# Grouped softmax: tiles of 384 rows in four buffers instead of 256 rows in six

## The chip, the cores and the metric

The kernel runs on one core of one Trainium2 chip. Times are device microseconds of one execution; the time of a kernel is the median of its runs. Before the change it is 1327.28 us (three runs, 1326.36 to 1327.6). The profile shows one execution, of 1324.7 us.

Three engines and the transfers matter here. VectorE (DVE in the profile) takes maxima and scales, ScalarE (ACT) takes exponentials, and two engines only issue transfers: SyncE (SP) the loads and GpSimd (POOL) most of the stores. The transfers themselves run on 16 DMA engines, which both queues share.

## What is computed

```python
def setup_inputs():
    B, N, D, G = 4, 4096, 4352, 8
    return {"x": np.random.randn(B, N, D).astype(np.float32)}

def reference(x):
    B, N, D = x.shape
    G = 8
    Dg = D // G
    x_g = x.reshape(B, N, G, Dg)
    x_g = x_g - x_g.max(axis=-1, keepdims=True)
    exp = np.exp(x_g)
    out = exp / exp.sum(axis=-1, keepdims=True)
    return out.reshape(B, N, D).astype(np.float32)
```

There are 4 x 4096 = 16,384 rows of 4352 float32 values (17,408 B). Each row is cut into eight groups of 544 values, and each group gets its own softmax. 285.2 MB are read and as many are written.

## The kernel before

A tile is 256 rows: each of the 128 partitions holds R = 2 whole rows that lie next to each other in memory, 34,816 B, and one DMA packet brings them. There are 64 tiles, and NT = 6 buffers that are used in turn. A tile is loaded into its buffer, worked on in place, and stored from it; the buffer is loaded again once its store has landed.

```python
    R = 2
    NT = 6
    RG = R * G
    ...
    xt = xf.rearrange("(t p r) d -> t p (r d)", p=P, r=R)
    ...
    bufs = [ctx.enter_context(nc.sbuf_tensor(f"xt{b}", [P, R * D], f32)) for b in range(NT)]
    ...
    parts = [(t, slice(0, RG)) for t in range(nt - 1)]
    parts += [(nt - 1, slice(r * G, (r + 1) * G)) for r in range(R)]
```

A part is a whole tile (16 groups per partition); only the last tile is done as two parts of one row each. VectorE takes the negated maxima of a part in one instruction, and later the reciprocals of the sums and the scaling, one instruction each:

```python
    def vector_max(n):
        t, g = parts[n]
        i = nc.vector.reduce_max(
            out=mx[:, t % NT, g], in_=groups(t, g), axis=X, negate=True)
        if g.start == 0:
            i.wait_op(landed[t % NT], 16 * (t // NT + 1), "sem-ge")
        ...
        i.then_inc(max_done, 1)

    def vector_scale(n):
        t, g = parts[n]
        nc.vector.reciprocal(out=rs[:, t % NT, g], in_=sm[:, t % NT, g]).wait_op(
            exp_done, n + 1, "sem-ge").then_inc(rec_done, 1)
        xg = groups(t, g)
        nc.vector.tensor_tensor(
            out=xg,
            in0=xg,
            in1=rs[:, t % NT, g].unsqueeze(2).to_broadcast([P, g.stop - g.start, Dg]),
            op=mybir.AluOpType.mult,
        ).wait_op(rec_done, n + 1, "sem-ge").then_inc(scaled, 1)
```

ScalarE takes one activation per group: exp(x - max), with the sum of the group as a second output.

```python
    def scalar_exp(n, count):
        ...
        for g in range(gs.start, gs.stop):
            i = nc.scalar.activation(
                out=xg[:, g - gs.start, :], in_=xg[:, g - gs.start, :], func=Exp,
                bias=mx[:, t % NT, g:g + 1], scale=1.0,
                accum_out=sm[:, t % NT, g:g + 1])
            if g == gs.start:
                i.wait_op(max_done, count, "sem-ge")
        i.then_inc(exp_done, 1)
```

The order is: SyncE issues all loads, each after the store that frees its buffer, and the stores of the last two tiles; GpSimd issues the other stores. ScalarE runs in a loop over the six buffers. VectorE runs straight through all tiles, and takes the maxima of tile n + 1 ahead of the scaling of tile n, so that ScalarE has work while VectorE scales:

```python
    for t in range(nt):
        if t >= NT:
            nc.sync.wait_ge(stored[t % NT], 16 * (t // NT))
        ...
            nc.sync.dma_start(out=tile_in[:, :], in_=xt[t]).then_inc(landed[t % NT], 16)
        ...
    for t in range(nt - LAST):
        nc.gpsimd.wait_ge(scaled, t + 1)
        nc.gpsimd.dma_start(out=ot[t], in_=bufs[t % NT][:, :]).then_inc(stored[t % NT], 16)
    ...
    vector_max(0)
    for n in range(len(parts)):
        if n + 1 < len(parts):
            vector_max(n + 1)
        vector_scale(n)
```

Of the kernel before, what the change touches and what calls it, by code (L numbers as in the profile page):

```python
# [1 line left out]

# [4 lines left out]


@with_exitstack
def kernel(  # L10
    ctx: ExitStack,
    tc: tile.TileContext,
    x: bass.AP,
    out: bass.AP,
):
    nc = tc.nc
    G = 8
    P = 128
    R = 2
    NT = 6  # L20
    RG = R * G
    xf = x.flatten_outer_dims()
    of = out.flatten_outer_dims()
    N, D = xf.shape
    Dg = D // G
    nt = N // (P * R)
    LAST = 2
    FIRST = 2
    turns = (nt - 1 - FIRST) // NT
    f32 = mybir.dt.float32  # L30
    X = mybir.AxisListType.X
    Exp = mybir.ActivationFunctionType.Exp
    xt = xf.rearrange("(t p r) d -> t p (r d)", p=P, r=R)
    ot = of.rearrange("(t p r) d -> t p (r d)", p=P, r=R)

    landed = [tc.alloc_semaphore(f"landed{b}") for b in range(NT)]
    stored = [tc.alloc_semaphore(f"stored{b}") for b in range(NT)]
    last_landed = tc.alloc_semaphore("last_landed")
    last_stored = tc.alloc_semaphore("last_stored")


    max_done = tc.alloc_semaphore("max_done")
    exp_done = tc.alloc_semaphore("exp_done")
    rec_done = tc.alloc_semaphore("rec_done")
    scaled = tc.alloc_semaphore("scaled")

    ctx.enter_context(tc.tile_critical(  # L47
        sync_engine=mybir.EngineType.Pool, no_gpsimd_drain=True))
    bufs = [ctx.enter_context(nc.sbuf_tensor(f"xt{b}", [P, R * D], f32)) for b in range(NT)]
    mx = ctx.enter_context(nc.sbuf_tensor("mx", [P, NT, RG], f32))  # L50
    sm = ctx.enter_context(nc.sbuf_tensor("sm", [P, NT, RG], f32))
    rs = ctx.enter_context(nc.sbuf_tensor("rs", [P, NT, RG], f32))

    parts = [(t, slice(0, RG)) for t in range(nt - 1)]
    parts += [(nt - 1, slice(r * G, (r + 1) * G)) for r in range(R)]

    def groups(t, g):
        return bufs[t % NT][:, :].rearrange("p (g d) -> p g d", d=Dg)[:, g, :]

    def vector_max(n):  # L60
        t, g = parts[n]
        i = nc.vector.reduce_max(  # L62
            out=mx[:, t % NT, g], in_=groups(t, g), axis=X, negate=True)
        if g.start == 0:
            i.wait_op(landed[t % NT], 16 * (t // NT + 1), "sem-ge")
        else:
            i.wait_op(last_landed, 16, "sem-ge")
        i.then_inc(max_done, 1)

    def vector_scale(n):  # L70
        t, g = parts[n]
        nc.vector.reciprocal(out=rs[:, t % NT, g], in_=sm[:, t % NT, g]).wait_op(  # L72
            exp_done, n + 1, "sem-ge").then_inc(rec_done, 1)
        xg = groups(t, g)
        nc.vector.tensor_tensor(  # L75
            out=xg,
            in0=xg,
            in1=rs[:, t % NT, g].unsqueeze(2).to_broadcast([P, g.stop - g.start, Dg]),
            op=mybir.AluOpType.mult,
        ).wait_op(rec_done, n + 1, "sem-ge").then_inc(scaled, 1)  # L80

    def scalar_exp(n, count):
        t, gs = parts[n]
        xg = groups(t, gs)
        for g in range(gs.start, gs.stop):
            i = nc.scalar.activation(  # L86
                out=xg[:, g - gs.start, :],
                in_=xg[:, g - gs.start, :],
                func=Exp,
                bias=mx[:, t % NT, g:g + 1],  # L90
                scale=1.0,
                accum_out=sm[:, t % NT, g:g + 1],
            )
            if g == gs.start:
                i.wait_op(max_done, count, "sem-ge")
        i.then_inc(exp_done, 1)

    for t in range(nt):  # L100
        if t >= NT:
            nc.sync.wait_ge(stored[t % NT], 16 * (t // NT))
        tile_in = bufs[t % NT]
        if t < nt - 1:
            nc.sync.dma_start(out=tile_in[:, :], in_=xt[t]).then_inc(landed[t % NT], 16)  # L105
        else:
            for r in range(R):
                nc.sync.dma_start(
                    out=tile_in[:, r * D:(r + 1) * D], in_=xt[t, :, r * D:(r + 1) * D],
                ).then_inc(landed[t % NT] if r < R - 1 else last_landed, 16)  # L110
    for t in range(nt - LAST, nt):
        nc.sync.wait_ge(scaled, t + 1 if t < nt - 1 else len(parts))
        nc.sync.dma_start(out=ot[t], in_=bufs[t % NT][:, :]).then_inc(last_stored, 16)


    for t in range(nt - LAST):
        nc.gpsimd.wait_ge(scaled, t + 1)
        nc.gpsimd.dma_start(out=ot[t], in_=bufs[t % NT][:, :]).then_inc(stored[t % NT], 16)  # L118
    for t in range(nt - NT, nt - LAST):
        nc.gpsimd.wait_ge(stored[t % NT], 16 * (t // NT + 1))  # L120
    nc.gpsimd.drain()
    nc.gpsimd.wait_ge(last_stored, 16 * LAST)

    nc.scalar.preload_act_table(Exp)  # L124

    for n in range(FIRST):
        scalar_exp(n, n + 1)
    nc.scalar.sem_inc(max_done, -FIRST)
    with nc.scalar.Fori(0, turns):
        for k in range(NT):  # L130
            scalar_exp(FIRST + k, k + 1)
        nc.scalar.sem_inc(max_done, -NT)
    for k, n in enumerate(range(FIRST + turns * NT, len(parts))):
        scalar_exp(n, k + 1)


    vector_max(0)
    for n in range(len(parts)):
        if n + 1 < len(parts):
            vector_max(n + 1)  # L140
        vector_scale(n)


# [1 line left out]
_INS = ['x']  # L145
_OUTS = [((4, 4096, 4352), 'float32')]


# [23 lines left out]
```

## Time and profile before

| what | value |
|---|---|
| time, median of 3 runs | 1327.28 us |
| span of the profiled run | 1324.7 us |
| bytes moved, mean rate | 570.48 MB, 431 GB/s over the span |
| maxima of a two-row tile (VectorE) | 9219 ns each |
| scaling of a two-row tile (VectorE) | 9225 ns each |
| reciprocals of a two-row tile (VectorE) | 243 ns each |
| exponentials of one group (ScalarE) | 734 ns each, 1024 of them |
| load of a tile, issue to landing (median) | 32.4 us |
| store of a tile, issue to landing (median) | 51.5 us |

How to read it: the busy time of an engine is only the time of its instructions. An engine may be busy for most of the span and still not be what the others wait for. So one asks at every stage which wait ends last, and what would start earlier if it were shorter. A row of forty digits shows the busy share of forty equal slices of the span in tenths (9 is 90% or more). A queue's share is the time that its packets took, as a share of what 16 DMA engines could give in the span. In the lists of waits a line is "who waited for what: us in total, times, the longest".

### The profile page before, as it was taken

The page shows a single profiled execution, that of the slowest core. Times are in us where ns is not written, and L with a number is a line of the kernel's source. Part 1 is how long each engine was busy: PE and PEld are TensorE (multiplying, and loading weights), DVE is VectorE, ACT ScalarE, POOL GpSimd, SP SyncE. Part 2 cuts the span into 40 slices and gives each one's busy share as a digit, 9 for nine tenths or more (in the row PEclk, how much of TensorE's full clock was granted, in tenths as well). Part 3 has the DMA queues.
Part 4 walks back from the last instruction along what each step waited for, and adds up shares of the span by engine and source line. Part 5 has one row for each costly group of instructions (what it writes and reads, how often), then busy time and mean ns, then how long its engine had stood idle before and what let it go on. Part 6 is the DMA issues. An engine that isn't in the chain of part 4 may idle for free.

```text
span 1324.7 us, 2465 instructions
## 1 busy us (share of the span) xinstructions
DVE 1190.0 (90%) x195; ACT 757.4 (57%) x2049; POOL 33.3 (3%) x66
## 2 busy tenths in 40 slices
DVE  5999999988989889898898998988989889898893
ACT  3765566547456465564655646556465474654751
POOL 0000000000000000000000000000000000000000
DMA  9999999999999999999999999999999999999998
GB/s 404 421 434 433 432 432 434 434 432 431 435 435 432 430 434 437 432 432 432 436 434 430 433 435 433 431 433 435 433 433 431 434 436 432 431 432 437 432 432 372
DMA packets 18582, 570.48 MB, mean 431 GB/s; under 512 B 2064, under 2 KB 2064, under 8 KB 2064
## 3 DMA queue, kind: packets, MB, share of 16 engines
q1 hardware_dynamic: 9648, 294.13, 51.5%
q0 software_dynamic: 8928, 276.30, 48.3%
q14 instruction: 6, 0.05, 0.0%
HBM read 285.21 MB, written 285.21 MB: 431 GB/s over the span
## 4 chain that ended last, share of the span: by engine, by line
another core or an unknown queue 69%; DVE 20%; DMA 7%; ACT 1%; SPq 1%; issue 0%; POOLq 0%
DVE xt L75 10%; DVE mx L62 10%; DMA out_dram<-xt 4%; DMA xt<-in_x_dram 3%; ACT xt L86 1%; SPq L105 1%; DVE rs L72 0%; SPq L167 0%; POOLq L47 0%; POOLq L156 0%
## 5 line engine op out<-in xcount | busy, mean ns | idle before, releaser
L86 ACT ACTIVATE xt<-xt,mx 128x544 f32<-128x544 f32 x1024 | 750.1, 734 | 542.4 <-DVE mx L62 542.4
L62 DVE TENSOR_REDUCE mx<-xt 128x16 f32<-128x8704 f32 (+1 forms) x65 | 590.1, 9079 | 110.8 <-DMA xt<-in_x_dram 110.8
L75 DVE TENSOR_TENSOR xt<-xt,rs 128x8704 f32<-128x8704 f32 (+1 forms) x65 | 590.6, 9086 | 2.2
L86 ACT ACTIVATION_READ_ACCUMULATOR xt<-xt,mx 128x1 f32 x1024 | 191.6, 187 | 0.0
L118 POOL DMA_DIRECT2D out_dram<-xt x62 | 33.1, 534 | 1243.5 <-DVE xt L75 1243.5
L72 DVE RECIPROCAL rs<-sm 128x16 f32<-128x16 f32 (+1 forms) x65 | 15.7, 242 | 2.8 <-ACT xt L86 2.8
L124 ACT ACT_TABLE_LOAD x1 | 1.3, 1283 | 0.9 <-PEq L156 0.9
L156 POOL MEMSET const-float32-0.0<- 128x1 f32 x1 | 0.1, 98 | 0.2 <-issue 0.2
L156 POOL MEMSET const-bfloat16-1.0<- 128x1 bf16 x1 | 0.1, 101 | 0.0
L156 POOL MEMSET const-uint8-127<- 128x1 uint8 x1 | 0.1, 99 | 0.0
L156 POOL MEMSET const-float32-1.0<- 128x1 f32 x1 | 0.1, 98 | 0.0
## 6 DMA issues: line engine op xcount, KB each, us to landing
xt<-in_x_dram SPq DMA_DIRECT2D x63, 4352.0 KB, 32.4
out_dram<-xt POOLq DMA_DIRECT2D x62, 4352.0 KB, 51.5
out_dram<-xt SPq DMA_DIRECT2D x2, 4352.0 KB, 20.1
xt<-in_x_dram SPq DMA_DIRECT2D x2, 2176.0 KB, 35.1
```

The lines of the kernel that those rows point to most:

```text
L62: i = nc.vector.reduce_max(out=mx[:, t % NT, g], in_=groups(t, g), axis=X, negate=True)
L72: nc.vector.reciprocal(out=rs[:, t % NT, g], in_=sm[:, t % NT, g]).wait_op(exp_done, n + 1, "sem-ge").then_inc(rec_done, 1)
L75: nc.vector.tensor_tensor(out=xg, in0=xg, in1=rs[:, t % NT, g].unsqueeze(2).to_broadcast([P, g.stop - g.start, Dg]), op=mybir.AluOpType.mu ...
L86: i = nc.scalar.activation(out=xg[:, g - gs.start, :], in_=xg[:, g - gs.start, :], func=Exp, bias=mx[:, t % NT, g:g + 1], scale=1.0, accum ...
L105: nc.sync.dma_start(out=tile_in[:, :], in_=xt[t]).then_inc(landed[t % NT], 16)
L118: nc.gpsimd.dma_start(out=ot[t], in_=bufs[t % NT][:, :]).then_inc(stored[t % NT], 16)
L124: nc.scalar.preload_act_table(Exp)
L156: nc = _bacc.Bacc("TRN2", target_bir_lowering=False, num_devices=1)
```

## The change

A tile becomes 384 rows: three rows per partition, so a packet is 52,224 B. Four buffers take the place of six, with the same bytes in all (208,896 B per partition). 16,384 rows make 42 such tiles and a last one of 256 rows. VectorE works tile by tile: three row maxima, then for each row the reciprocals and the scaling. It no longer takes the next tile's maxima ahead. Maxima, sums and exponentials are signalled by row, the end of a tile's scaling by tile. VectorE and ScalarE both loop over the four buffers, ten turns of four tiles, and the last three tiles follow the loop. In VectorE's loop the semaphores are counted back in each turn. The last tile's load is no longer split in two.

The change is for larger packets and fewer transfers, with less code on VectorE.

```diff
-    R = 2
-    NT = 6
-    RG = R * G
+    R = 3
+    NT = 4
+    LAST = 2
...
+    rows = [R] * (N // (P * R))
+    if N > sum(rows) * P:
+        rows.append(N // P - sum(rows))
+    nt = len(rows)
+    turns = (nt - 1) // NT
...
+    def vector_tile(b, n_rows, landed_at, done):
+        for r in range(n_rows):
+            i = nc.vector.reduce_max(
+                out=of_row(mx, b, r), in_=groups(b, r), axis=X, negate=True)
+            if r == 0:
+                i.wait_op(landed[b], landed_at, "sem-ge")
+            i.then_inc(max_done, 1)
+        for r in range(n_rows):
+            nc.vector.reciprocal(out=of_row(rs, b, r), in_=of_row(sm, b, r)).wait_op(
+                exp_done, done + r + 1, "sem-ge").then_inc(rec_done, 1)
+            xg = groups(b, r)
+            i = nc.vector.tensor_tensor(
+                out=xg, in0=xg,
+                in1=of_row(rs, b, r).unsqueeze(2).to_broadcast([P, G, Dg]),
+                op=mybir.AluOpType.mult,
+            ).wait_op(rec_done, done + r + 1, "sem-ge")
+            if r == n_rows - 1:
+                i.then_inc(scaled, 1)
...
+    with nc.scalar.Fori(0, turns):
+        for b in range(NT):
+            scalar_tile(b, R, b * R)
+        nc.scalar.sem_inc(max_done, -NT * R)
...
-    vector_max(0)
-    for n in range(len(parts)):
-        if n + 1 < len(parts):
-            vector_max(n + 1)
-        vector_scale(n)
+    with nc.vector.Fori(0, turns):
+        for b in range(NT):
+            vector_tile(b, R, 16, b * R)
+            nc.vector.sem_inc(landed[b], -16)
+        nc.vector.sem_inc(exp_done, -NT * R)
+        nc.vector.sem_inc(rec_done, -NT * R)
+    for t in rest:
+        vector_tile(t % NT, rows[t], 16, first_row[t] - first_row[turns * NT])
```

More of the change, by code (lines that the diff above doesn't have):

```diff
@@ L25 @@
     Dg = D // G
[L26 to L29, printed above, removed]
     f32 = mybir.dt.float32
@@ L32, with dram @@
     Exp = mybir.ActivationFunctionType.Exp
-    xt = xf.rearrange("(t p r) d -> t p (r d)", p=P, r=R)
-    ot = of.rearrange("(t p r) d -> t p (r d)", p=P, r=R)
+    rows = [R] * (N // (P * R))
[3 more added lines that the diff above has]
+    turns = (nt - 1) // NT
+    first_row = [sum(rows[:t]) for t in range(nt + 1)]
+    def dram(a, t):
+        lo, hi = first_row[t] * P, first_row[t + 1] * P
+        return a[lo:hi, :].rearrange("(p r) d -> p (r d)", p=P)
     landed = [tc.alloc_semaphore(f"landed{b}") for b in range(NT)]
     stored = [tc.alloc_semaphore(f"stored{b}") for b in range(NT)]
-    last_landed = tc.alloc_semaphore("last_landed")
     last_stored = tc.alloc_semaphore("last_stored")
@@ L49 @@
     bufs = [ctx.enter_context(nc.sbuf_tensor(f"xt{b}", [P, R * D], f32)) for b in range(NT)]
[L50 to L96, printed above, removed]
+    mx = ctx.enter_context(nc.sbuf_tensor("mx", [P, NT, R * G], f32))
@@ new lines, with groups, of_row @@
+    sm = ctx.enter_context(nc.sbuf_tensor("sm", [P, NT, R * G], f32))
+    rs = ctx.enter_context(nc.sbuf_tensor("rs", [P, NT, R * G], f32))
+    def groups(b, r):
+        return bufs[b][:, r * D:(r + 1) * D].rearrange("p (g d) -> p g d", d=Dg)
+    def of_row(a, b, r):
+        return a[:, b, r * G:(r + 1) * G]
+    def vector_tile(b, n_rows, landed_at, done):
[16 more added lines that the diff above has]
+                i.then_inc(scaled, 1)
@@ L100, with scalar_tile @@
+    def scalar_tile(b, n_rows, done):
+        for r in range(n_rows):
+            xg = groups(b, r)
+            for g in range(G):
+                k = r * G + g
+                i = nc.scalar.activation(
+                    out=xg[:, g, :], in_=xg[:, g, :], func=Exp,
+                    bias=mx[:, b, k:k + 1], scale=1.0, accum_out=sm[:, b, k:k + 1])
+                if g == 0:
+                    i.wait_op(max_done, done + r + 1, "sem-ge")
+            i.then_inc(exp_done, 1)
     for t in range(nt):
@@ L102 @@
             nc.sync.wait_ge(stored[t % NT], 16 * (t // NT))
[L103 to L110, printed above, removed]
+        nc.sync.dma_start(
+            out=bufs[t % NT][:, :rows[t] * D], in_=dram(xf, t)).then_inc(landed[t % NT], 16)
     for t in range(nt - LAST, nt):
-        nc.sync.wait_ge(scaled, t + 1 if t < nt - 1 else len(parts))
-        nc.sync.dma_start(out=ot[t], in_=bufs[t % NT][:, :]).then_inc(last_stored, 16)
+        nc.sync.wait_ge(scaled, t + 1)
+        nc.sync.dma_start(
+            out=dram(of, t), in_=bufs[t % NT][:, :rows[t] * D]).then_inc(last_stored, 16)
     for t in range(nt - LAST):
         nc.gpsimd.wait_ge(scaled, t + 1)
-        nc.gpsimd.dma_start(out=ot[t], in_=bufs[t % NT][:, :]).then_inc(stored[t % NT], 16)
+        nc.gpsimd.dma_start(
+            out=dram(of, t), in_=bufs[t % NT][:, :rows[t] * D]).then_inc(stored[t % NT], 16)
     for t in range(nt - NT, nt - LAST):
@@ L122 @@
     nc.gpsimd.wait_ge(last_stored, 16 * LAST)
+    rest = range(turns * NT, nt)
     nc.scalar.preload_act_table(Exp)
-    for n in range(FIRST):
-        scalar_exp(n, n + 1)
-    nc.scalar.sem_inc(max_done, -FIRST)
     with nc.scalar.Fori(0, turns):
[L130 to L134, printed above, removed]
-    vector_max(0)
-    for n in range(len(parts)):
-        if n + 1 < len(parts):
-            vector_max(n + 1)
-        vector_scale(n)
+        for b in range(NT):
+            scalar_tile(b, R, b * R)
+        nc.scalar.sem_inc(max_done, -NT * R)
+    for t in rest:
+        scalar_tile(t % NT, rows[t], first_row[t] - first_row[turns * NT])
+    with nc.vector.Fori(0, turns):
[4 more added lines that the diff above has]
+        nc.vector.sem_inc(rec_done, -NT * R)
+    for t in rest:
+        vector_tile(t % NT, rows[t], 16, first_row[t] - first_row[turns * NT])
 _INS = ['x']
```

## The prediction

> **What bounds the kernel now.** I read the head of the page first: the span, how long each engine works, and how evenly.
>
> ```profile
> span 1324.7 us, 2465 instructions
> ...
> DVE 1190.0 (90%) x195; ACT 757.4 (57%) x2049; POOL 33.3 (3%) x66
> ...
> DMA  9999999999999999999999999999999999999998
> ...
> q1 hardware_dynamic: 9648, 294.13, 51.5%
> q0 software_dynamic: 8928, 276.30, 48.3%
> ```
>
> VectorE works 90% of the span, but the DMA row is full in 39 of 40 slices, and the packets of the two queues took 51.5 + 48.3 = 99.8% of 16 engines' span. The transfers are the bound. The question for VectorE is whether it still has slack. The waits, and the groups kept apart by shape, say how much:
>
> ```profile
> POOL out_dram L118 <- DVE xt L75: 1243.5, 62, 44.4
> ACT xt L86 <- DVE mx L62: 542.4, 64, 21.0
> DVE mx L62 <- DMA xt<-in_x_dram: 110.8, 51, 13.9
> ```
>
> Columns: who waited, for what, us in total, times, longest. VectorE waits for loads 51 times, 13.9 us for the first tile and (110.8 - 13.9) / 50 = 1.94 us for each later one. It never waits for a store, and ScalarE only waits for it. The stretches of the run (us, then busy time of each engine, clock, DMA share, GB/s) show that this holds from the start to the last stores:
>
> ```profile
> 3.00:110.00 107.00, 93.28 (x16) 59.65 (x162) 2.26 (x4) 1.00 1.00 427
> 110.00:1220.00 1110.00, 1016.35 (x164) 649.14 (x1760) 29.23 (x55) 1.00 1.00 433
> 1220.00:1290.00 70.00, 65.88 (x12) 41.41 (x112) 1.60 (x3) 1.00 1.00 432
> 1290.00:1306.00 16.00, 14.49 (x6) 5.96 (x16) 0.00 (x0) 1.00 1.02 440
> 1306.00:1320.00 14.00, 0.00 (x0) 0.00 (x0) 0.00 (x0) 1.00 0.97 420
> ```
>
> Even the computation of the last tile, which ends near 1306 us, lies beside stores that are still queued. By the records of single packets the first one starts at 1.90 us and the last ends at 1322.78 us. So the span is 1.9 us of start, 1320.9 us of packets without a gap, and 1.9 us of end. The median time is 2.6 us above the profiled span; I carry that over.
>
> **What the Trainium skill says.** "DMA: Bandwidth & Descriptors", section "Where 436 GB/s comes from", puts the ceiling of the 16 ports at 435.2 GB/s. The trace agrees: 433 GB/s in the long middle stretch. So a better overlap has nothing to win; only less work per byte can. The same page, "Queues, rings and completion order", says that each DMA engine goes round-robin between the rows that have work, packet by packet. The trace fits: the two queues took nearly equal shares. I use it for the way in which loads and stores share the engines. "Advanced Engine Details and Errata", section "Control Flow Timing", gives about 108 ns for a compare-and-branch. ScalarE's loop in this trace shows 45 ns for one in the record, and its activations keep their 0.73 us rhythm across it (one starts at 151.55, 152.28, 153.01 us, with the branch between). That bears on VectorE's new loop.
>
> **Part 1: larger packets.** A load or store moves one packet per partition. The records show 1288 ns for a packet of 34,816 B and 648 ns for one of 17,408 B (the halves of the last tile). So 17,408 B cost 640 ns and a packet has 8 ns of its own; a packet of 52,224 B should take 1288 + 640 = 1928 ns. Before there are 127 transfers of 128 large packets (63 loads, 64 stores) and two half loads: 16,256 + 256 = 16,512 packets. After, 16384 / 384 gives 42 tiles and a rest of 256 rows: 43 loads and 43 stores of 128 packets, 11,008. That saves 5,504 x 8 ns / 16 engines = 2.8 us. Each transfer also ends with a small packet of 9 ns on every engine: 129 before, 86 after, 43 x 9 ns = 0.4 us saved. Sum: 3.2 us less of DMA work, 0.24% of the time, and all of it on the path, because the path is DMA.
>
> **Part 2: VectorE's order.** It may not exceed the DMA time of a tile, which is 16 packets of 1.928 us on each engine (8 in, 8 out) and two small ones, 30.87 us. The durations per row are in the trace, since the last tile is done by rows (first the groups: busy time, mean ns, idle time before; then the end of the timeline: start, us):
>
> ```profile
> L75 DVE TENSOR_TENSOR xt<-xt,rs 128x4352 f32<-128x4352 f32 x2 | 9.4, 4694 | 0.1
> L62 DVE TENSOR_REDUCE mx<-xt 128x8 f32<-128x4352 f32 x2 | 9.4, 4680 | 0.0
> ```
>
> ```profile
> 1290.11 4.68 DVE L62 TENSOR_REDUCE mx<-xt 128x8 f32<-128x4352 f32 x1
> 1294.70 0.20 DVE L72 RECIPROCAL rs<-sm 128x8 f32<-128x8 f32 x1
> 1294.93 4.69 DVE L75 TENSOR_TENSOR xt<-xt,rs 128x4352 f32<-128x4352 f32 x1
> ```
>
> From start to start a row's maximum costs 1294.70 - 1290.11 = 4.59 us (records overlap by 0.09), its reciprocal 0.23, its scaling 4.69 less the same overlap. Three rows: 3 x (4.59 + 0.23 + 4.60) = 28.3 us. Before, a two-row tile takes 18.55 (maxima start at 62.97 and 81.52 us), or 27.8 for three rows. So shorter instructions cost VectorE 0.5 us per tile, inside a slack that falls from 3.1 (1.5 x the 20.6 us rhythm, less 27.8) to 2.6 us.
>
> The new order gives up the maximum of the next tile that used to run during ScalarE's exponentials. Does VectorE now wait for ScalarE? Eight exponentials take 8 x 0.731 = 5.85 us. With the first maximum ending at 4.65, the rows' exponentials end at 10.5, 16.4 and 22.2 us. VectorE ends its maxima at 13.8 and wants the sums at 13.8, 18.6 and 23.5. Each is there at least 1.3 us earlier. No wait, and ScalarE has 30.9 - 17.6 us to spare. The loop adds a few semaphore and register instructions per tile and a branch per four tiles, by the 45 ns above under 0.5 us per tile even if nothing hides them.
>
> **Part 3: four buffers.** The bytes on the chip are the same, 6 x 34,816 = 4 x 52,224 B per partition, and the round is the same 4 x 30.87 = 123.5 us. In that round a buffer is 28.3 us with VectorE, and some 8 us, as my estimate, go into issue, first packet and completion (store 0 is issued at 44.8 us and its first packet starts at 49.7; the first load is issued at 0.9 and its first packet starts at 1.9). That leaves 87 us for load and store, which need 31 us each when they share the engines. So about 2.8 of the four buffers are in the queues, and the engines have work.
>
> The two ends are tight. *Start*: the first load lands 5.1 us later (8 packets x 0.64), at 19.0; VectorE ends tile 0 at 47.3 and tile 1 at 75.6. The four loads and store 0 are 5 x 15.43 = 77.2 us of work from 1.9, with slow first packets (1.8 to 2.4 us) done at 79.7. Store 1 is issued at 76.1 and begins up to 4.9 us later, as store 0 did before, and load 4 waits for store 0's completion. So between 0 and 2 us of idle DMA engines. *End*: the load of the last tile lands while VectorE still works on tile 41. From there two maxima, the second row's exponentials and its scaling take 4.65 + 11.7 + 0.25 + 4.7 = 21.3 us, and its store begins some 2 us later. Store 41 covers 15.4 us of these 23.3, so 8 us must come from stores queued before. Because stores wait for their turn (median to landing 51.5 us before, against 32.4 for loads), I expect about 13 us of queue: no gap, with a few us of margin. If the queue is empty instead, the gap is 8 us.
>
> **Sum.** 1327.3 - 3.2 + 1.3 (my allowance for both ends) = 1325.4 us.
>
> **Rivals.** (a) *VectorE becomes the bound*: maxima first and scalings after could leave it waiting for ScalarE. Then a tile takes 4.65 + 17.6 + 4.9 = 27.2 us at the least by ScalarE's chain, 28.3 by its own work, against 30.87. For it: the slack is only 2.6 us, and a hidden cost of 3.5 us a tile would make 43 x 0.9 = 39 us, 1365 in all. Against: every term is measured, and they leave no such cost. (b) *Buffers too coarse*: a quarter of the memory is now bound in computation at a time, and a tile frees its buffer only at the end of its store. A gap of 1 us per tile makes 1367. For it: the load queue will run dry for moments. Against: an engine is idle only if both queues are dry, and 2.8 buffers are there. (c) *Only the ends lose*: the full 2 + 8 us make 1327.3 - 3.2 + 10 = 1334. This is the rival I take most seriously. (d) *The granularity gains more than 8 ns a packet*: the packets' times add up to the whole span already, so there is nothing else to win; at best 1323.5.
>
> **Range and chances.** The saving is firm and small; the losses are one-sided and bounded by (c), so I say 1322 to 1333 us. Faster by 2% would need 26 us, where DMA can give 3: 0.005. Slower by 2% needs (a) or (b) in strength: 0.02. Within 2%: 0.975.
>
> **What would show it.** Packets of 52,224 B at 1928 ns and a DMA row full to the end confirm part 1. Maxima of consecutive tiles 30.9 us apart with 2 to 3 us of waiting for loads, and hardly any waiting of the reciprocals for ScalarE, confirm part 2. VectorE never waiting for loads, or 28.3 growing to 31, would be rival (a); a DMA share under 0.99 in the long middle stretch rival (b); a share well under 1 around 80 us or in the last 30 us rival (c). I am wrong if the large packets take other than 1928 ns, or if a loop's cost appears that ScalarE's loop doesn't show.

## The result and the profile after

The changed kernel takes 1333.41 us (median of four runs, 1328.91 to 1336.64), the kernel before 1326.84 beside it. The ratio is 1.0048, with a 95% interval of [1.0025, 1.0071]. That is within 2%, as forecast, but slower rather than 0.1% faster, and 0.4 us above the upper end of the predicted range. The runs also lie further apart than the four of the kernel before: 7.7 us from the fastest to the slowest, against 1.2.

The head of the page of the changed kernel, with the DMA row, the two queues' shares, and the median times from issue to landing:

```profile
span 1333.5 us, 2690 instructions
...
DVE 1206.1 (90%) x384; ACT 755.1 (57%) x2049; POOL 22.1 (2%) x45
...
DMA  9999999999999999999999999999999999999987
...
q1 hardware_dynamic: 6480, 296.36, 51.6%
q0 software_dynamic: 5904, 274.07, 47.5%
...
xt<-in_x_dram SPq DMA_DIRECT2D x42, 6528.0 KB, 38.7
out_dram<-xt POOLq DMA_DIRECT2D x41, 6528.0 KB, 56.3
```

The queues' shares add up to 99.1% of the span; before it was 99.8%. The DMA row is full until the last two slices. The same stretches as before (busy time of VectorE, ScalarE, GpSimd, then clock, DMA share, GB/s) show where the difference is:

```profile
3.00:110.00 107.00, 90.51 (x29) 54.23 (x147) 1.73 (x3) 1.00 1.00 429
110.00:1220.00 1110.00, 1024.12 (x326) 642.40 (x1747) 19.12 (x36) 1.00 1.00 433
1220.00:1290.00 70.00, 64.87 (x23) 43.72 (x119) 1.06 (x2) 1.00 1.00 434
1290.00:1306.00 16.00, 15.96 (x5) 5.37 (x17) 0.00 (x0) 1.00 0.67 289
1306.00:1320.00 14.00, 10.65 (x5) 8.11 (x23) 0.00 (x0) 1.00 0.64 277
```

Up to 1290 us nothing is missing, and then a third of the transfers' time is. The waits and one stretch of VectorE's timeline say that its own part went as planned: a tile from 524.25 to 552.6 us, 2.8 us of waiting for the next load, and reciprocals that wait for ScalarE only twice in the run, in the last tile.

```profile
DVE mx L64 <- DMA xt<-in_x_dram: 106.2, 34, 19.2
DVE rs L70 <- ACT xt L86: 2.4, 2, 1.4
```

```profile
524.25 13.87 DVE L64 TENSOR_REDUCE mx<-xt 128x8 f32<-128x4352 f32 x3 [2.78 <-DMA xt<-in_x_dram]
...
547.94 4.69 DVE L73 TENSOR_TENSOR xt<-xt,rs 128x4352 f32<-128x4352 f32 x1
555.47 4.69 DVE L64 TENSOR_REDUCE mx<-xt 128x8 f32<-128x4352 f32 x1 [2.84 <-DMA xt<-in_x_dram]
```

**Where the time went.** I took the packet records apart. They don't name the engine, but in this trace a packet starts 3 to 4 ns before the one ahead of it on the same engine ends, so 16 chains can be followed, apart from a few swaps. In the tail 15 chains stop twice: from about 1293 to 1299 us, when store 40 is done on them and VectorE has not finished tile 41 (its last scaling starts at 1292.98), and from 1314 to 1320, when store 41 is done and tile 42 is not. The 16th chain never stops. It ends store 40 at 1312 us, 18 us after most others, store 41 at 1321.9, and the last store at 1331.8.

That engine did not fall behind in the tail. Each landing leaves 16 records, one per engine, and the time from the first to the last of them tells how far the engines have drifted apart (with the latest engine left out in brackets):

| store that lands near | before, us | changed, us |
|---|---|---|
| 110 us | 2.3 (2.2) | 5.0 (0.7) |
| 300 us | 3.1 (2.3) | 5.7 (2.1) |
| 610 us | 3.0 (2.3) | 13.3 (3.9) |
| 890 us | 3.0 (2.2) | 19.2 (6.2) |
| 1200 us | 3.7 (2.8) | 23.3 (6.8) |

The chain that is late has no long gaps either. Its *load packets are longer*: where the others take 1928 ns, some 40 of its 344 take 1960 to 2740. Between 60 and 1240 us this adds 11.5 us on that chain, and at most 2.7 on any other. A count over all engines needs no chains: from 200 to 1240 us, 81 load packets are stretched by over 30 ns, 18.6 us in all. In the kernel before there is not one. A tile is used only when its load has landed on all engines, and a buffer is free only when its store has. So the latest engine set the pace, 31.04 us per tile from landing to landing (the loads of tiles 12 to 40) in place of the 30.87 that I had worked out. The 15 others worked off their queued stores meanwhile, and had nothing left to hide the last tile's computation behind.

So there are two suspects, the late engine and the tail, and for the late engine four possible causes: chance, the software queue of the stores, too little slack in four buffers, the large packets. Fourteen experiments were made to tell them apart.

### The profile page after: what moved, and what is told of

It is laid out like the page before. It is cut to its first block, busy times and chain, and to the rows that moved or that the text cites. A ratio compares the mean times of both kernels' runs of the same rounds, so it can differ in the third digit from the quotient of the medians.

```text
span 1333.5 us, 2690 instructions
## 1 busy us (share of the span) xinstructions
DVE 1206.1 (90%) x384; ACT 755.1 (57%) x2049; POOL 22.1 (2%) x45
## 3 DMA queue, kind: packets, MB, share of 16 engines
q0 software_dynamic: 5904, 274.07, 47.5%
## 4 chain that ended last, share of the span: by engine, by line
another core or an unknown queue 71%; DVE 16%; DMA 8%; issue 2%; ACT 1%; SPq 1%; DVEq 0%; POOLq 0%
DVE mx L64 9%; DVE xt L73 7%; DMA xt<-in_x_dram 4%; DMA out_dram<-xt 4%; ACT xt L86 1%; SPq L96 1%; DVE rs L70 0%; DVEq L122 0%; SPq L155 0%; POOLq L49 0%; DVEq L127 0%; DVEq L126 0%; POOLq L144 0%
## 5 line engine op out<-in xcount | busy, mean ns | idle before, releaser
L64 DVE TENSOR_REDUCE mx<-xt 128x8 f32<-128x4352 f32 x128 | 591.8, 4679 | 106.2 <-DMA xt<-in_x_dram 106.2
L73 DVE TENSOR_TENSOR xt<-xt,rs 128x4352 f32<-128x4352 f32 x128 | 600.5, 4692 | 4.4
L105 POOL DMA_DIRECT2D out_dram<-xt x41 | 21.9, 534 | 1245.3 <-DVE xt L73 1245.3
L70 DVE RECIPROCAL rs<-sm 128x8 f32<-128x8 f32 x128 | 24.9, 195 | 2.4 <-ACT xt L86 2.4
## 6 DMA issues: line engine op xcount, KB each, us to landing
xt<-in_x_dram SPq DMA_DIRECT2D x42, 6528.0 KB, 38.7
out_dram<-xt POOLq DMA_DIRECT2D x41, 6528.0 KB, 56.3
out_dram<-xt SPq DMA_DIRECT2D x1, 4352.0 KB, 13.1
```

Source lines behind the costliest of these rows:

```text
L64: i = nc.vector.reduce_max(out=of_row(mx, b, r), in_=groups(b, r), axis=X, negate=True)
L70: nc.vector.reciprocal(out=of_row(rs, b, r), in_=of_row(sm, b, r)).wait_op(exp_done, done + r + 1, "sem-ge").then_inc(rec_done, 1)
L73: i = nc.vector.tensor_tensor(out=xg, in0=xg, in1=of_row(rs, b, r).unsqueeze(2).to_broadcast([P, G, Dg]), op=mybir.AluOpType.mult,).wait_o ...
L105: nc.gpsimd.dma_start(out=dram(of, t), in_=bufs[t % NT][:, :rows[t] * D]).then_inc(stored[t % NT], 16)
```

## The experiments

Letters for the theories: A, the late engine sets the end; B, the tail does; C, the software queue makes an engine late; D, too little slack does; E, the packets' size does; G, the addresses do; H, being out of step does. Experiments 1 to 4 ran on one chip, 5 to 8 and 12 to 14 on a second, 9 to 11 on a third; what this leaves open is said under "Together".

### 1. The changed kernel again

No edit.

> The changed kernel once more, untouched, to see whether what its first trace shows comes back. There, one of the 16 DMA engines fell behind the others: the last of the 16 landings of a store came 2.5 us after the first for tile 0 and 23 us after it for tile 38, and the load packets of that engine were stretched (some 40 of 344 took 1.96 to 2.74 us in place of 1.928), about 11 us in all. Theory A (one engine falls behind, and the end waits for it): the spread of store landings grows again to 10 us or more, and the time goes with the size of that spread, 1329 to 1337 us. Theory B (the late engine was an accident, the tail of the program is the loss): spread under 5 us in this trace, two gaps of about 6 us in the last 40 us all the same, time 1328 to 1334.

Measured: 1336.39 us, nine runs from 1325.36 to 1338.55, ratio 1.0055 [1.0034, 1.0076]. Three runs lie under 1329 and five at 1336 or above. The profiled run was one of the short ones (1327.32 us), and its landings drift less: 1.8 us near 110, 5.6 at 610 and 914, 7.4 at 1192. Ten load packets are stretched between 200 and 1240 us (1.7 us), where the first trace had 81. The stretches of its end:

```profile
1290.00:1306.00 16.00, 13.61 (x5) 11.81 (x32) 0.00 (x0) 1.00 1.06 457
1306.00:1320.00 14.00, 4.71 (x2) 0.00 (x0) 0.00 (x0) 1.00 0.76 325
```

Same program, and the engines are busy through 1306 us; after that 14 of them stop once, for 1.5 to 4.1 us. So the two gaps of 6 us are not fixed by the program: in these two traces they grow with the drift. The tile's rhythm is 30.82 us here. The latest engine never stops for as much as 1 us in either trace. Its stretched loads add 4.2 us between 60 and 1240 us here and 11.5 there, and its last packet ends at 1323.5 us here and at 1331.8 there: most of the 8.3 us is the stretching. This fits A. B, which needs the two gaps in any run, doesn't fit. The kernel before has long runs too, but rarely: four of its 46 in this batch are over 1334 us, and two of its 65 in the later batches over 1333. No trace of one was kept, so what makes those long is not known.

### 2. The last stores row by row

```diff
+            if last:
+                i.then_inc(row_scaled, 1)
...
-        nc.sync.wait_ge(scaled, t + 1)
-        nc.sync.dma_start(out=dram(of, t), in_=bufs[t % NT][:, :rows[t] * D]).then_inc(last_stored, 16)
+        for r in range(rows[t]):
+            nc.sync.wait_ge(row_scaled, first_row[t] - first_row[nt - LAST] + r + 1)
+            nc.sync.dma_start(out=dram(of, t)[:, r * D:(r + 1) * D],
+                              in_=bufs[t % NT][:, r * D:(r + 1) * D]).then_inc(last_stored, 16)
```

> Only the tail is changed: the last two tiles are stored row by row (17,408 B packets), each row as soon as it is scaled, so both gaps of the DMA engines in the tail (1293 to 1299 us and 1314 to 1319 us) can be filled. Theory A (the late engine sets the end; it has no gap in the tail): the other 15 engines end earlier, the late one does not, gain at most 2 us against the changed kernel. Theory B (the tail sets the end): gain of 5 to 10 us against the changed kernel, to 1323 to 1327 us.

Measured: 1330.71 us, 22 runs from 1325.25 to 1338.23, ratio 1.0026 [1.0007, 1.0046]; 5.7 us below run 1 by the medians. But both kernels' runs are spread over the same 13 us, and their medians are loose; the means of all runs are 1333.3 and 1331.1, 2.2 apart. The ends of the two ranges are the same to 0.4 us. So filling the gaps doesn't take away the long runs, which B needs, and a gain of 5 us is not excluded either. In the profiled run (1332.11 us) 62 loads are stretched, by 15.1 us in all, and two engines are late together, 15 us behind the first from 610 us on. I count this one for A, not as a proof.

### 3. Stores on a hardware queue

```diff
-    for t in range(nt - LAST):
-        nc.gpsimd.wait_ge(scaled, t + 1)
-        nc.gpsimd.dma_start(...)
+    for t in range(nt):
+        scalar_tile(t % NT, rows[t], first_row[t])
+        if t < nt - LAST:
+            nc.scalar.wait_ge(scaled, t + 1)
+            nc.scalar.dma_start(...).then_inc(stored[t % NT], 16)
```

> The stores of all tiles but the last two are issued by ScalarE, on a hardware queue, in place of GpSimd's software queue; ScalarE runs straight through and issues a tile's store after the wait for its scaling, where it had nothing to do anyway. Theory C (the software queue makes one engine late): the spread of store landings stays at 3 us or less, few stretched packets, time 1323 to 1327 us. Theory A with another cause (buffers too few, or large packets): the spread grows as before, time 1329 to 1337 us.

Measured: 1336.8 us, five runs from 1335.41 to 1338.85, ratio 1.0081 [1.0068, 1.0094]. Store landings are 10.1 us apart near 114 us and 23.1 at 615, and 119 loads are stretched (29.5 us). C falls as the cause. The Trainium skill ("DMA: Bandwidth & Descriptors", section "Latency and other measured facts") gives, as a best guess, the software queue's descriptor rings as the reason why two of the engines are usually slower than the others. Here two engines are late without that queue, 22.4 and 23.1 us behind the first near 615 us; the records don't say which two.

### 4. Less work per tile

Left out: exponentials, reciprocals and scaling of rows 1 and 2 of each tile, which are stored as loaded.

```diff
-        for r in range(n_rows):            # reciprocal and scaling
+        for r in range(1):
...
-        for r in range(n_rows):            # exponentials
+        for r in range(1):
```

> The changed kernel with less work in each tile: exponentials, reciprocals and scaling are left out for rows 1 and 2 (their values are stored as they were loaded), maxima of all rows stay. A buffer is then about 19 us with VectorE in place of 28.3, so 9 us more per round are left for queues; packets, tiles and buffers are the same. Theory D (the buffers' slack is too small, a queue of an engine runs dry, and that makes one engine late): no growth of the spread, stretched packets nearly gone after the start, time 1322 to 1325 us. Theory E (the packets of 52,224 B themselves are what makes one engine late): spread grows to 10 us or more as before, time within 4 us of the changed kernel's less what the shorter tail saves (about 7 us).

Measured: 1324.59 us, 20 runs, ratio 0.9991 [0.9979, 1.0004]. Fifteen runs lie between 1323.98 and 1325.8, the other five between 1327.6 and 1334.6. The profiled run is the longest, and in it the spread of the store landings grows from 1.5 us near 106 to 12.3 at 1195, with 95 stretched loads (19.4 us). So with more slack long runs are rarer (5 of 20), and the late engine still comes. D alone doesn't explain it. The tail is shorter too in this kernel, so its times can't be set against those of the changed kernel one to one.

### 5. Three small packets in place of a large one

```diff
-        return a[lo:hi, :].rearrange("(p r) d -> p (r d)", p=P)
+        return a[lo:hi, :].rearrange("(r p) d -> p r d", p=P)
```

> The changed kernel with the same tiles, buffers and order, but the three rows of a partition lie 128 rows apart in memory, so each transfer has three packets of 17,408 B per partition in place of one of 52,224. The packets alone then take 2048 x 0.648 = 1327.1 us per engine in place of 1317.8, 9.3 us more. Theory E (large packets make an engine late): stretched load packets nearly gone (under 2 us on the worst engine, 4 to 9 us in the changed kernel's traces), the runs lie close together, 1333 to 1336 us. Theory D (the four buffers leave too little slack, whatever the packets): stretched packets and a spread of the runs of 8 us or more stay, median 1338 to 1348 us.

Measured: 1330.34 us, eight runs from 1329.85 to 1330.74, ratio 1.0028 [1.0018, 1.0039]. Between 200 and 1240 us no load is stretched, and the landings of a store stay 1.5 to 1.8 us apart to the end. E predicts this: without the large packets the spread and the stretched packets are gone. The time is 3 us below what I expected, since small packets cost less than their records say (see the reckoning below).

### 6. Five buffers of the old size

```diff
-    NT = 6
+    NT = 5
```

> The kernel before with five of its 256-row buffers in place of six; packets (34,816 B), order and the rest stay. Theory D (slack): a round is 5 x 20.6 = 103 us, of which VectorE holds a buffer for about 39 and issue and completion take some 8, so 56 us are left for load and store that need 41; the slack falls from 36 to 15 us, below the 25 of the changed kernel. Then stretched load packets after the start appear (over 3 us on the worst engine) and the runs spread as in the changed kernel, median 1328 to 1337 us. Theory E (large packets): stretched packets stay at the level of the kernel before (0.6 us on the worst engine), median 1326 to 1328 us.

Measured: 1328.27 us, 21 runs from 1327.51 to 1329.92, ratio 1.0013 [1.0007, 1.002]. No load is stretched between 200 and 1240 us; the landings of a store drift from 2.8 to 4.6 us. The long middle stretch has the full rate of 433 GB/s. With less slack than the changed kernel by my estimate (15 us against 25) there is no late engine and no wide range of times, so too few buffers alone don't make one.

### 7. and 8. The parts of the change apart

The old look-ahead with the new tiles, and the new order with the old tiles:

```diff
-    with nc.vector.Fori(0, turns): ...          # three maxima, three scalings
+    vector_max(0, rows[0], 16)
+    for t in range(nt):
+        if t + 1 < nt:
+            vector_max((t + 1) % NT, rows[t + 1], 16 * ((t + 1) // NT + 1))
+        vector_scale(t % NT, rows[t], first_row[t])
```

```diff
-    R = 3
-    NT = 4
+    R = 2
+    NT = 6
```

> The changed kernel with the old look-ahead: VectorE takes the three row maxima of tile n+1 before the scalings of tile n, and runs straight through; tiles, packets and four buffers are as changed. A buffer is then with VectorE for two tiles' work, about 56 us and the wait for the next load. Of the round of 123.5 us some 57 are left for load and store, which need 62 when they share the engines. Theory D: slower than the changed kernel by 1 to 5% (a queue runs dry in each round), 1345 to 1400 us. If the slack doesn't matter at all: 1325 to 1337 us like the changed kernel.

> The new order of VectorE with the old tiles: 256 rows, six buffers, 34,816 B packets, VectorE in the new loop without look-ahead. With two rows VectorE must wait for ScalarE: a tile takes 4.65 (first maxima) + 2 x 5.85 (exponentials of two rows) + 0.25 + 4.7 = 21.3 us, against 20.6 for its transfers. So VectorE bounds: 64 x 21.3 + 14 (first load) + 12 (last store) + 3 = 1392 us, with reciprocals waiting about 1.4 us and 0.9 us for ScalarE in each tile as in the last tile of the changed kernel. If the order cost nothing in itself, 1325 to 1328 us.

Measured: 1421.02 us for the look-ahead (four runs from 1405.33 to 1435.7, ratio 1.0649 [1.0598, 1.0701]) and 1398.74 us for the old tiles (four runs from 1398.6 to 1399.01, 1.0543 [1.0527, 1.0559]). Here are the long middle stretch and the waits of the first:

```profile
110.00:1220.00 1110.00, 953.75 (x305) 592.88 (x1613) 18.06 (x34) 1.00 0.98 406
```

```profile
DVE mx L64 <- DMA xt<-in_x_dram: 190.0, 39, 19.5
```

and the wait that bounds the second:

```profile
DVE rs L70 <- ACT xt L86: 150.9, 128, 1.4
```

The look-ahead holds two of four buffers, the transfers fall to 406 GB/s, and the kernel is slower by more than I expected (1345 to 1400): the direction is that of D, the size isn't. With two rows the new order waits for ScalarE in all 128 rows, 150.9 us in all, where the three-row order waits twice. So new tiles and new order depend on each other; each alone costs over 5%.

### 9. Small packets at the old addresses

```diff
-    bufs = [... ([P, R * D], f32) ...]
+    bufs = [... ([P, R, D + 8], f32) ...]
```

> The changed kernel, its rows in memory as there (three neighbouring rows per partition, 52,224 B apart from partition to partition), but the rows of a buffer lie 32 B apart on the chip, so that each transfer falls into three packets of 17,408 B per partition in place of one of 52,224. The run before this, with three packets of rows that lay 128 rows apart in memory, had no late engine and 1329.9 to 1330.7 us; packet size and addresses had changed together there. Theory E (the packets' size makes an engine late): again no stretched load packets after 150 us and runs within 2 us of each other, 1329 to 1332 us. Theory G (the addresses, with engines 4 x 52,224 B apart in memory, make an engine late): stretched load packets of 4 us or more on the worst engine, and runs spread over 8 us or more, 1330 to 1343.

Measured: 1330.37 us, seven runs from 1329.98 to 1332.44, ratio 1.0027 [1.0016, 1.0038]; no stretched load after 200 us, landings of a store 1.5 to 2.1 us apart. G falls: with the same places in memory and small packets there is no late engine.

### 10. and 11. Only the loads small, only the stores small

```diff
-        nc.sync.dma_start(out=bufs[t % NT][:, :rows[t] * D], in_=dram(xf, t)).then_inc(landed[t % NT], 16)
+        for r in range(rows[t]):
+            nc.sync.dma_start(out=bufs[t % NT][:, r * D:(r + 1) * D],
+                              in_=dram(xf, t)[:, r * D:(r + 1) * D]).then_inc(landed[t % NT], 16)
```

The other kernel does the same to the stores that GpSimd issues, and leaves the loads whole.

> The changed kernel with each load issued as three loads, one per row (packets of 17,408 B); stores keep their packets of 52,224 B, addresses are as in the changed kernel. The stretched packets were all load packets. If large load packets are what goes wrong: no late engine, runs within 3 us of each other, 1327 to 1330 us. If large store packets beside them are what makes load packets wait: load packets of 0.648 us are stretched in the same way, worst engine 4 us or more, runs spread over 8 us or more.

> The changed kernel with each of the GpSimd stores issued as three stores, one per row (packets of 17,408 B); loads keep their packets of 52,224 B. If large load packets are what goes wrong: one engine late as in the changed kernel, worst engine 4 us or more of stretched load packets, runs spread over 8 us or more, 1327 to 1342 us. If large store packets are the cause: no late engine, runs within 3 us of each other, 1327 to 1331 us. In both cases a load now takes about twice the turns of a store, since the engines go round packet by packet, so loads should land sooner and stores later.

Measured: 1377.65 us (1370.58 to 1389.25, ratio 1.0392 [1.0351, 1.0434]) and 1377.95 us (1377.55 to 1380.15, ratio 1.0387 [1.0373, 1.04]). Neither expectation holds: both lose 50 us. First the transfers of the kernel with small loads, then its middle stretch:

```profile
xt<-in_x_dram SPq DMA_DIRECT2D x128, 2176.0 KB, 43.5
out_dram<-xt POOLq DMA_DIRECT2D x41, 6528.0 KB, 26.2
```

```profile
110.00:1220.00 1110.00, 987.76 (x315) 617.28 (x1678) 18.60 (x35) 1.00 1.00 424
```

and the transfers of the kernel with small stores:

```profile
xt<-in_x_dram SPq DMA_DIRECT2D x42, 6528.0 KB, 26.6
out_dram<-xt POOLq DMA_DIRECT2D x123, 2176.0 KB, 35.1
```

The whole tile's store lands in 26.2 us beside small loads, where it took 56.3 in the changed kernel, and the whole tile's load in 26.6 beside small stores, where it took 38.7. The side with the large packets is served faster. This is what turns packet by packet give, as the Trainium skill says ("DMA: Bandwidth & Descriptors", section "Queues, rings and completion order"): at equal turns the side with three times the bytes per packet gets three quarters of the engine. The order of the packets agrees: followed from 200 to 1200 us, 89 and 90% of the large ones, one record each, are followed by one of the other queue. (The nearly equal shares of the two queues, which the prediction took as agreement, don't show it: both queues move the same number of bytes.) So these two runs don't tell which side's size makes an engine late; they unbalance the queues as well. They do show one thing about reading: the DMA share is 1.00, while the rate is 424 GB/s and not 433. A stretched packet counts as busy. Between 200 and 1240 us 838 and 1207 loads are stretched in these two, 786 and 1181 in runs 7 and 8, the last with packets of 34,816 B. So in these four kernels, whose queues run empty or unbalanced, stretched packets come at each size that was tried and on all 16 engines. With filled and balanced queues only the packets of 52,224 B were stretched all through the run.

### 12. and 13. One engine made late on purpose

One extra load of 127 partitions x 2048 B ahead of all others, in the kernel before and in the kernel of run 9:

```diff
+    nc.sync.dma_start(out=bufs[NT - 1][:127, :512], in_=xf[:127, :512]).then_inc(kicked, 16)
     for t in range(nt):
+        if t == NT - 1:
+            nc.sync.wait_ge(kicked, 16)
```

> The kernel before, and ahead of its loads one extra load of 127 partitions x 2048 B (260 KB, 0.05% of the bytes) into the buffer that is loaded last, which is loaded again with its own data after that. Such a load should go to one DMA engine alone, so that this engine starts some 10 us behind the other 15. Theory A (the end waits for the latest engine): 5 to 10 us slower than the kernel before, 1331 to 1337 us. Theory H (an engine that is out of step gets its load packets stretched): beyond that its delay grows on, over 3 us of stretched load packets on it, 1338 us or more. If neither holds: 1326 to 1329 us, the delay is absorbed.

> The kernel of 384-row tiles with three packets of 17,408 B per partition (rows 32 B apart on the chip, 1330.4 us), with the same extra load of 260 KB on one engine ahead of the others. Theory A: 5 to 10 us slower than without it, 1335 to 1341 us. Theory H: the engine that was put out of step gets its load packets stretched by over 3 us and falls further behind, 1342 us or more. If small packets keep the engines from being slowed even out of step: the delay stays at about 10 us or shrinks, and no stretched packets appear on that engine.

Measured: 1337.2 us (1336.76 to 1342.44, ratio 1.0079 [1.0065, 1.0092]) and 1341.09 us (1340.98 to 1341.22, ratio 1.0109 [1.0093, 1.0124]), that is 10.7 us more than without the extra load in both. Its 127 packets follow one another for 13.4 and 13.1 us. In the first kernel the first tile's load lands 10.2 us later on that engine than on the first, and for the loads from 200 us to the last it is 10 to 11 us; no packet is stretched between 400 and 1100 us. (The profiled run was the longest of the five; its 46 stretched loads all lie before 400 us.) In the second kernel the engines come back to within 3.3 us of each other, and there are no stretched packets from 200 us on. So it is shown by itself that one late engine makes the kernel late, which is what A needs: 0.05% of the bytes, all on one engine, cost 0.8% of the time. And H falls for packets of 34,816 and 17,408 B: the engine stays out of step in the first kernel, and after 400 us that stretches no packets.

### 14. The size between

```diff
-        return a[lo:hi, :].rearrange("(p r) d -> p (r d)", p=P)
+        return a[lo:hi, :].rearrange("r d -> (r d)").rearrange("(h p e) -> p h e", h=2, p=P)
```

> The changed kernel with the rows of a tile dealt out in halves: each partition holds two pieces of one and a half rows (12 groups each, so every group is whole) that lie apart in memory, two packets of 26,112 B in place of one of 52,224. The size between the two that were run. Theory E with a threshold between 34,816 and 52,224 B: no late engine, runs within 2 us of each other, 1327 to 1330 us. If the late engine comes gradually with size: worst engine 2 us or more of stretched load packets and runs over 3 us apart.

Measured: 1328.88 us, 20 runs from 1328.75 to 1329.18, ratio 1.0012 [1.0004, 1.0019]. Not one run in 20 is long. The landings of a store are 3.7 us apart from 300 to 1200 us, and from 200 to 1240 us no load is stretched. The stretches of its end, to be held against those of the changed kernel:

```profile
1220.00:1290.00 70.00, 64.77 (x21) 38.02 (x104) 1.44 (x2) 1.00 1.00 432
1290.00:1306.00 16.00, 14.49 (x5) 10.96 (x30) 0.00 (x0) 1.00 0.99 426
1306.00:1320.00 14.00, 4.89 (x2) 0.86 (x4) 0.00 (x0) 1.00 0.90 386
```

Tiles, buffers, order, loops and tail are those of the changed kernel; only the packets are half as large, and the tail's gaps are nearly gone (0.99 and 0.90, for 0.67 and 0.64 in the first trace of the changed kernel and 1.06 and 0.76 in its short run).

### Together

| kernel | chip | packets | runs, us | profiled span, us | stretched loads, 200 to 1240 us | spread of a store landing near 1200 us |
|---|---|---|---|---|---|---|
| before | all three | 34,816 B | 1326.1 to 1328.1; 6 of 115 from 1333.5 to 1346.6 | 1324.7 | none | 3.7 us |
| five old buffers | second | 34,816 B | 1327.5 to 1329.9 | 1326.5 | none | 4.6 us |
| rows apart in memory | second | 3 x 17,408 B | 1329.9 to 1330.7 | 1327.8 | none | 1.8 us |
| rows apart on the chip | third | 3 x 17,408 B | 1330.0 to 1332.4 | 1328.3 | none | 2.1 us |
| pieces of a row and a half | second | 2 x 26,112 B | 1328.8 to 1329.2 | 1327.0 | none | 3.7 us |
| changed, again (a short run) | first | 52,224 B | 1325.4 to 1338.6 | 1325.2 | 10, 1.7 us | 7.4 us |
| last stores by row | first | 52,224 B | 1325.3 to 1338.2 | 1330.0 | 62, 15.1 us | 15.1 us |
| changed | not recorded | 52,224 B | 1328.9 to 1336.6 | 1333.5 | 81, 18.6 us | 23.3 us |
| less work per tile (a long run) | first | 52,224 B | 1324.0 to 1334.6 | 1332.5 | 95, 19.4 us | 12.3 us |
| stores on a hardware queue | first | 52,224 B | 1335.4 to 1338.9 | 1333.6 | 119, 29.5 us | 23.2 us |

In the four traces of kernels that compute the whole result with packets of 52,224 B, the span goes with the spread: 7.4, 15.1, 23.3 and 23.2 us go with 1325.2, 1330.0, 1333.5 and 1333.6 us. That is the case for A.

Among kernels whose loads and stores stayed balanced, the wide range of times came with the packets of 52,224 B, and long runs were the rule there: 9 of the 13 runs of the changed kernel are over 1331 us. But one thing was not kept apart from the packets: *the chip*. Of the balanced kernels, those with packets of 52,224 B that ran on a known chip all ran on the first, and those with smaller ones on the second and third; only the kernel before ran on all three, and its runs are alike there apart from the few long ones (4 of 46 on the first chip, 2 of 65 on the others). So the first chip doesn't make every kernel late. That it makes this one late, with the packets as a bystander, was not tried: the changed kernel was not run beside the kernels of small packets. E is the likeliest reading, and not proved. *Why* a packet of 52,224 B is sometimes stretched on one or two engines stays open in any case. It is not the software queue and not too few buffers alone, and the addresses and being out of step did no harm at the smaller sizes. That an engine out of step is stretched at 52,224 B, so that a small delay feeds itself, would fit the steady growth in the table of landings; it was not tried. None of the kernels that compute the whole result is shown faster than the kernel before.

## Why the prediction missed

**Bound.** Right: DMA before and after, VectorE waiting for loads and never the reverse.

**Part 1, larger packets.** A packet of 52,224 B does take 1928 ns on most engines (stores 1928.5 on average, loads 1937.3). The saving was over-sized. I took 8 ns as a packet's own cost from two durations. But packets overlap by 3 to 4 ns on an engine, so the own cost has to be read from a rhythm: from landing to landing (the loads of tiles 12 to 40) a tile takes 30.82 us with 16 packets on each engine (the short run), 30.88 with 32 (run 14) and 30.98 with 48 (run 9), 4 to 5 ns per packet. 5,504 packets fewer at 5 ns on 16 engines are 1.7 us, not 2.8.

**The step that failed** is in the same part: "all of it on the path, because the path is DMA". I reckoned with 16 engines as with one server that moves 16 packets a tile in 30.87 us. The landing waits for the latest of 16, and in the changed kernel one of them falls behind by stretched loads, 11.5 us on that engine alone. Against the short run that cost 31.04 - 30.82 = 0.22 us a tile, over 42 tiles about 9 us; the two profiled spans (1333.5 and 1325.2) are 8.3 us apart. That the packets' size is what stretches them is likely and not proved. "What would make me wrong" named packets other than 1928 ns; it was right as a warning, but I had given it no weight in the range.

**Part 2, VectorE's order.** Right in every term. A tile takes 75.77 - 47.48 = 28.29 us (28.3), waits of 2.4 to 3.2 us for most loads (2.6 expected), no waits for ScalarE before the last tile, and no cost of the loop that would show in these starts. (The branch that I placed between activations near 152 us is at 154.01 us in that trace, and took 50 ns there; most others took 45. The rhythm of 0.73 us holds across it.)

**Part 3, four buffers.** The start was right: first load at 19.18 us (19.0), tile 0 done at 47.5 (47.3), and no gap of the DMA engines around 80 us that amounts to 0.4 us (0 to 2 expected). At the end the last tile took 1319.07 - 1297.59 = 21.5 us (21.3). But the 13 us of queued stores that I expected to cover it were there for one engine only. The median of 56.3 us from issue to landing, like the 51.5 of before that I argued from, is the time of the latest engine; on the other 15 the queue was empty.

**Rivals.** (a) and (b) did not come about. (c), "only the ends lose", gives the number, 1334, by coincidence, for the reason was another: without a late engine the ends cost little, as the tail of the kernel with half-size packets shows (a DMA share of 0.99 and 0.90). The run at 1325.36 lies on my sum of 1325.4, but it is the fastest of 13, and the sum holds a saving of 3.2 us that was not there in full. The range had a fault of its own: I called (c) the most serious rival and put it at 1334, and closed the range at 1333.

## What to carry to other kernels

When the DMA share is near 1.00, look at the spread of the 16 landings of a transfer, not only at its last one: a landing waits for the latest engine, and a few us on one engine are a few us of the kernel. Saving a packet's own cost was worth at most 1.7 us here, so packets beyond the size at which runs lie close together were not worth having; give loads and stores that share engines packets of equal size. Read a packet's cost from the rhythm of landings and not from its record.

## What was not expected of the hardware

- Packets of 52,224 B gave times 13 us apart for one and the same program on one chip (1325.4 to 1338.6), packets of 26,112 B times 0.4 us apart in 20 runs on another.
- Loads of 17,408 B packets beside stores of 52,224 B, or the reverse, cost 3.9% at a DMA share of 1.00; equal sizes of 17,408 B on both sides cost 0.3%.
- A load of 127 partitions x 2048 B went to one engine and took 13 us, and delayed the whole kernel by 10.7 us.
